# Attention scores of an encoder trunk: three products of 96 rows, or one of 32 and two of 128

## The chip, the cores and the metric

The kernel runs on one core of one Trainium2 chip. The metric is the device time of one execution in microseconds, as a median over runs. The core has five engines that follow their own instruction streams and meet at semaphores: TensorE (PE in the profile, with its weight loads as PEld), VectorE (DVE), ScalarE (ACT), GpSimd (POOL) and SyncE (SP), which here only issues transfers. TensorE reads its operands from SBUF and writes to PSUM, of which a core has eight banks of 128 partitions by 512 float32 values.

## The reference

Two layers act on a residual stream of 512 rows and 1024 columns. Each layer normalises, projects, runs three mixers side by side (latent attention, pooling, gating), projects back, and ends with a gated feed-forward part. The change touches the attention mixer alone:

```
s = (jnp.einsum('bqhd,bkhd->bhqk', qn, k_nope)
     + jnp.einsum('bqhr,bkr->bhqk', qr, k_rope))
p = jax.nn.softmax(s.astype(jnp.float32) * scale, axis=-1).astype(v.dtype)
return jnp.einsum('bhqk,bkhd->bqhd', p, v)
```

There are 8 heads. A score is a sum over 96 terms: 64 of a part without position (`nope`, its own key for each head) and 32 of a rotated part (`rope`, one key that all heads share). Queries go in four blocks of 128, keys are 512.

## The kernel before, in words

**Two parts for each number.** Operands of TensorE are split into a high part (rounded to the type `float32r`) and a low part (the rest). A product of two split operands takes three passes: high by high, high by low, low by high (`mm3`, line 538). A tile that holds both parts is a "unit" of 128 partitions, two slots and 512 columns, named `u` in the profile.

**Attention before the change.** `pair(pr)` makes the keys and queries of two heads: 15 products of 128 rows, then for each head ScalarE writes the high part and VectorE the low part into partitions 0 to 63 of the head's units `kh` and `qh`, slot 0 and slot 1, and two transfers by SyncE put both parts of the rotated key and query into partitions 64 to 95. `score(i)` then handles tile `i`, that is head `i // 4` and query block `i % 4`: three passes of 96 rows into one PSUM bank, then the softmax (VectorE's maximum, ScalarE's exponential with its sum, VectorE's reciprocal, and the scaling on VectorE or GpSimd). `turn(i)` transposes the probabilities on TensorE and splits them, and `weigh(n)` multiplies two turned tiles with the values. There are 32 tiles in a layer. `AHEAD = 4`, `WLAG = 2` and `PAIR = 4` say by how many tiles these steps are written apart; other work (`BESIDE`: gating, pooling, and `out_early`, the first half of the output projection) is written between them.

**What sets the order.** Nothing is issued as it is written. A recording layer (`Program`) takes every operation down, and `order` (line 330) places them: engine by engine it takes the operation that can start earliest by its own table of costs (`_cost`, line 233) and lags, and among those the one whose successors are due first. PSUM has three pools, "s" with three banks (scores), "p" with three (turned probabilities and weighted values) and "b" with two. Operations written with `either` go to VectorE, or to GpSimd where the planner sees them end early enough there. All instructions are issued from one line (493), so the profile tells them apart by their tiles: `ps` is a PSUM bank, `t` a tile of 512 columns, `s` the softmax's small numbers, `wu` split weights, `raw` weights as loaded.

**Queues.** SyncE's transfers stand in one queue, in the planner's order: a transfer that waits for its source holds back those behind it, weight loads too.

Of the kernel before, what the change touches and what calls it, by code (L numbers as in the profile page):

```python
# [16 lines left out]
ALU = mybir.AluOpType  # L17
AX = mybir.AxisListType

P = 128  # L20
D = 1024
T = 512
NT = T // P
# [3 lines left out]
NOPE = 64  # L27
ROPE = 32
# [188 lines left out]
class Op:  # L217
# [15 lines left out]
    def _cost(self, engine):  # L233

        n = self.out.free() if isinstance(self.out, View) else 0
        if self.method == "tensor_reduce":
            n = max(x.free() for x in self.reads)
        if self.method == "dma_start":
            return 1.0 if engine == "gpsimd" else 0.06
        if engine == "tensor":  # L240
            return {1: 0.213, P: 0.109}.get(n, n / 2400 + 0.0135)
        vectors = sum(isinstance(self.kw.get(k), View) for k in ("bias", "scale", "scalar", "scalar1", "accum_out"))
        from_psum = any(x.buf.pool.psum for x in self.reads)
        if engine == "scalar":
            return (0.05 if from_psum else 0.09) + n / 1200 + 0.093 * vectors
        if engine == "gpsimd":
            if self.kw.get("op") == ALU.pow:
                return 0.3 + n * 0.165
            return 0.15 + n * 0.0021 if self.method == "tensor_tensor" else 0.05 + n * 0.0013
        if self.method == "reciprocal":  # L250
            return 0.08 + n * 0.008
        fast = self.method in ("tensor_copy", "tensor_scalar") and not from_psum
        return 0.07 + n / (1920 if fast else 960) + 0.06 * vectors
# [245 lines left out]
def encoder(ctx: ExitStack, tc: tile.TileContext, wts, xT, pos, cols, sgn, fin, cst, rc, out):  # L499
    nc = Program(tc)  # L500
# [34 lines left out]
    def f32(ap):  # L535
        return ap.bitcast(F32)
# [167 lines left out]
    for l in range(DEPTH):  # L704
# [213 lines left out]
        def k_rotary():  # L918
            wr = unit()[:, 0].rearrange("p (k c) -> p k c", c=2 * ROPE)
            raw = load(l, 8)  # L920
            rraw = raw[:, : KD * ROPE].rearrange("p (k c) -> p k c", c=ROPE)
            nc.scalar.activation(wr[:, :, :ROPE], rraw, AF.Copy)
            nc.vector.tensor_tensor(out=wr[:, :, ROPE:], in0=rraw, in1=f32(wr[:, :, :ROPE]), op=ALU.subtract)
            rot_parts["w"] = split(raw, 768, None, 256)
            ps = bank("b")
            for k in range(KD):
                nc.tensor.matmul(ps[: 2 * ROPE], wr[:, k], xg[k][:, 0], start=(k == 0), stop=False)
                nc.tensor.matmul(ps[: 2 * ROPE], wr[:, k], xg[k][:, 1], start=False, stop=(k == KD - 1))
            kr = tmp()
            nc.scalar.copy(out=kr[:ROPE], in_=ps[ROPE : 2 * ROPE])  # L930
            nc.vector.tensor_tensor(out=kr[:ROPE], in0=kr[:ROPE], in1=ps[:ROPE], op=ALU.add)
            nc.vector.tensor_tensor(out=kr[:ROPE], in0=kr[:ROPE], in1=rs["bc"][:ROPE], op=ALU.mult)
            rot_parts["k"] = rotate(kr, ROPE)

        def rotate(src, n):

# [93 lines left out]
        def pair(pr):  # L1030
            w = weights(l, 14 + pr, nc.either)
            pk = bank("b")
            for k in range(KKV):
                s = slice(k * P, (k + 1) * P)
                mm3(pk[:], w[:, 0, s], w[:, 1, s], ckv[k][:, 0], ckv[k][:, 1], k == 0, k == KKV - 1)
            pq = bank("b")
            for k in range(KQ):
                s = slice((KKV + k) * P, (KKV + k + 1) * P)
                mm3(pq[:], w[:, 0, s], w[:, 1, s], cq[k][:, 0], cq[k][:, 1], k == 0, k == KQ - 1)
            for j in range(2):  # L1040
                h = 2 * pr + j
                kh, qh = unit(), unit()
                rows = slice(j * NOPE, (j + 1) * NOPE)
                for dst, src in ((kh, pk), (qh, pq)):
                    nc.scalar.activation(dst[:NOPE, 0], src[rows], AF.Copy)
                    nc.vector.tensor_tensor(
                        out=dst[:NOPE, 1], in0=src[rows], in1=f32(dst[:NOPE, 0]), op=ALU.subtract
                    )
                nc.sync.dma_start(f32(kh[NOPE:E]), f32(rot_parts["k"][:ROPE]))
                qrow = slice((h % 4) * ROPE, (h % 4 + 1) * ROPE)  # L1050
                nc.sync.dma_start(f32(qh[NOPE:E]), f32(qrot[h // 4][qrow]))
                heads[h] = (kh, qh)

        probs, pts = {}, {}

        def score(i):
            h, t = divmod(i, NT)
            kh, qh = heads[h]
            ts_ = slice(t * P, (t + 1) * P)
            ps = bank("s")  # L1060
            mm3(ps[:], qh[:E, 0, ts_], qh[:E, 1, ts_], kh[:E, 0], kh[:E, 1], True, True)
            st = small("att")
            nc.vector.tensor_reduce(out=st[:, 0:1], in_=ps[:], axis=AX.X, op=ALU.max, negate=True)
            pe = tmp()
            nc.scalar.activation(pe[:], ps[:], AF.Exp, bias=st[:, 0:1], accum_out=st[:, 2:3])
            nc.vector.reciprocal(out=st[:, 3:4], in_=st[:, 2:3])
            nc.either.tensor_scalar(
                out=pe[:], in0=pe[:], scalar1=st[:, 3:4], scalar2=1.0, op0=ALU.mult, op1=ALU.mult
            )
            probs[i] = pe  # L1070

        def turn(i):
            pe = probs.pop(i)
            if i % 2 == 0:
                pth, ptl = unit(), unit()
                pts[i // 2] = [x[:].rearrange("p a (k q) -> p (a k) q", q=256) for x in (pth, ptl)]
            pth3, ptl3 = pts[i // 2]
            pt = bank("p")
            for kt in range(NT):
                nc.tensor.transpose(pt[:, kt * P : (kt + 1) * P], pe[:, kt * P : (kt + 1) * P], ident[:])  # L1080
            pt3 = pt[:].rearrange("p (k q) -> p k q", q=P)
            qs = slice((i % 2) * P, (i % 2 + 1) * P)
            nc.scalar.activation(pth3[:, :, qs], pt3, AF.Copy)
            nc.vector.tensor_tensor(out=ptl3[:, :, qs], in0=pt3, in1=f32(pth3[:, :, qs]), op=ALU.subtract)

        fulls = {}

        def weigh(n):
            h, qp = divmod(n, 2)
            pth3, ptl3 = pts.pop(n)  # L1090
            po = bank("p")
            for kt in range(NT):
                nc.tensor.matmul(po[:, :256], vt[kt][:, h], pth3[:, kt], start=(kt == 0), stop=False)
# [40 lines left out]
        for i in range(max(n_tiles + AHEAD + WLAG, max(BESIDE) + 1)):  # L1134
            if i < n_tiles:
                if i % 8 == PAIR and i // 8 + 1 < HEADS // 2:
                    pair(i // 8 + 1)
                score(i)
            j = i - AHEAD
            if 0 <= j < n_tiles:  # L1140
                turn(j)
            for name in BESIDE.get(i, ()):
                jobs[name]()
            j = i - AHEAD - WLAG
            if j >= 0 and j % 2 == 1:
                weigh(j // 2)


        acc = tpool.tile([P, T], F32, tag="acc", name=nm("acc"), bufs=2)
# [555 lines left out]
```

## Time and profile before

| | us |
|---|---|
| median of 3 runs | 1097.53 (1097.27 to 1097.63) |
| the profiled execution's own time | 1096.46 |
| its span, first to last instruction | 1094.7 |
| attention of the first layer, first to last score | 92.7 to 167.1 |
| attention of the second layer | 635.4 to 709.8 |

The profile is one execution. Its page gives each engine's busy time; matmuls are pipelined and their ends are modelled, so a busy TensorE is not one at its peak, and the pace of products is read from the starts of groups in the timeline. A row of a groups view has the line, engine, operation and tiles, count, busy time, mean of one, and what the engine waited for ahead of it. A row of the windows view has the stretch, then for each engine its busy time and instructions.

### The profile page before, as it was taken

How to read it: one execution, taken by the hardware profiler on the slowest of the kernel's cores; microseconds unless marked ns; L12 is line 12 of the kernel's file. 1: busy time of each engine (PE TensorE's matmuls, PEld its weight loads, DVE VectorE, ACT ScalarE, POOL GpSimd, SP SyncE). 2: the span in 40 equal slices, each digit the busy share in tenths (PEclk: the TensorE clock that was granted, in tenths of full speed). 3: DMA queues.
4: the chain of work that ended last, by engine and by line, in shares of the span. 5: the costliest groups of instructions: out<-in, count | busy, mean ns of one | idle time of the engine just before them, and what ended most of it. 6: DMA issues, size and time to landing. Idle time of an engine off the chain costs nothing.

```text
span 1094.7 us, 14521 instructions
## 1 busy us (share of the span) xinstructions
PE 1070.3 (98%) x5324; PEld 900.6 (82%) x5324; DVE 864.6 (79%) x1196; ACT 648.8 (59%) x995; POOL 170.5 (16%) x198
## 2 busy tenths in 40 slices
PE   9999899999999999999999998999999999999997
PEld 7787688888888999887887877888888889998885
DVE  7679996898876778994556899969977866799963
ACT  6357784775565555662353677847755655666642
POOL 0217320101001100020001273201001001100201
PEclk9999999999999999999999999999999999999999
DMA  6333214656546547385132422155567356563922
GB/s 214 101 100 94 69 44 152 190 148 141 140 131 134 118 133 227 101 221 130 58 116 75 129 66 63 59 203 144 157 151 172 97 126 144 137 209 102 259 64 97
DMA packets 44392, 142.71 MB, mean 130 GB/s; under 512 B 5744, under 2 KB 6000, under 8 KB 44320
## 3 DMA queue, kind: packets, MB, share of 16 engines
q1 hardware_dynamic: 33936, 108.05, 29.7%
q0 software_dynamic: 9808, 32.67, 16.9%
q10 hardware_dynamic: 576, 1.05, 0.3%
q8 instruction: 42, 0.69, 0.2%
q14 instruction: 30, 0.25, 0.1%
HBM read 135.33 MB, written 2.23 MB: 126 GB/s over the span
## 4 chain that ended last, share of the span: by engine, by line
PE 84%; DVE 8%; issue 4%; ACT 3%; DMA 1%; POOL 1%; POOLq 0%; DVEq 0%; ACTq 0%
PE ps L493 84%; DVE u L493 4%; DVE t L493 2%; DVE s L493 1%; ACT u L493 1%; ACT t L493 1%; DVE wu L493 1%; ACT wu L493 1%; DMA wr<-in_wts 0%; DVE vz L493 0%; DMA u<-u 0%; ACT vm L493 0%; DVE z L493 0%; POOL u L493 0%; POOL r L493 0%
## 5 line engine op out<-in xcount | busy, mean ns | idle before, releaser
L493 PE MATMUL ps<-wu,xp 128*128 128x512 f32 (+1 forms) x2976 | 658.7, 380 | 2.4 <-ACT wu L493 2.0
L493 PEld LDWEIGHTS ps<-wu,xp 128*128 128x128 f32 x2976 | 547.0, 188 | 93.0 <-ACT wu L493 2.3
L493 ACT ACTIVATE wu<-wr 128x1024 fp32r<-128x1024 f32 (+1 forms) x224 | 225.3, 1008 | 200.1 <-PE ps L493 162.6
L493 DVE TENSOR_TENSOR wu<-wr,wu 128x1024 fp32r<-128x1024 f32 (+1 forms) x224 | 258.3, 1156 | 92.2 <-ACT wu L493 91.4
L493 PE MATMUL ps<-u,wu 128*128 128x512 f32 x972 | 236.6, 395 | 2.5 <-DVE wu L493 1.7
L493 PEld LDWEIGHTS ps<-u,wu 128*128 128x128 f32 x972 | 178.6, 188 | 42.3 <-DVE wu L493 3.2
L493 POOL DMA_DIRECT2D wr<-in_wts x64 | 55.9, 983 | 561.5 <-DVE wr L493 201.3
L493 PE MATMUL ps<-u,u 128*128 128x256 f32 (+3 forms) x516 | 107.0, 344 | 4.2 <-ACT t L493 2.6
L493 ACT ACTIVATE wu<-raw 128x1024 fp32r<-128x1024 f32 (+3 forms) x66 | 63.1, 959 | 65.1 <-PE ps L493 40.0
L493 ACT COPY t<-ps 128x512 f32<-128x512 f32 (+3 forms) x124 | 62.2, 503 | 47.5 <-PE ps L493 43.9
L493 PEld LDWEIGHTS ps<-u,u 128*128 128x128 f32 (+2 forms) x516 | 74.6, 186 | 18.3 <-ACT t L493 4.3
L493 DVE TENSOR_TENSOR wu<-raw,wu 128x1024 fp32r<-128x1024 f32 (+3 forms) x60 | 67.6, 1130 | 27.1 <-ACT wu L493 26.6
L493 DVE TENSOR_TENSOR wr<-wr,wr 128x1024 f32<-128x1024 f32 (+1 forms) x64 | 73.7, 1154 | 4.8 <-DMA wr<-in_wts 4.4
L493 DVE TENSOR_TENSOR u<-ps,u 128x512 fp32r<-128x512 f32 (+1 forms) x104 | 70.0, 683 | 6.1 <-ACT u L493 5.1
L493 ACT ACTIVATE u<-ps 128x512 fp32r<-128x512 f32 (+1 forms) x104 | 61.2, 596 | 15.6 <-PE ps L493 14.3
L493 DVE TENSOR_TENSOR t<-ps,t 128x512 f32<-128x512 f32 (+2 forms) x92 | 50.4, 567 | 20.7 <-PE ps L493 16.2
L493 ACT ACTIVATE t<-ps,s 128x512 f32<-128x512 f32 x64 | 43.8, 688 | 9.4 <-DVE s L493 7.8
L493 POOL TENSOR_SCALAR t<-t,s 128x512 f32<-128x512 f32 x54 | 37.8, 705 | 66.1 <-DVE s L493 49.6
L493 PE MATMUL ps<-ident,t 128*128 128x128 f32 x288 | 43.7, 274 | 4.0 <-DVE t L493 2.1
L493 PEld LDWEIGHTS ps<-ident,t 128*128 128x128 f32 x288 | 34.0, 140 | 15.1 <-issue 5.0
L493 DVE TENSOR_TENSOR res<-ps,res 128x512 f32<-128x512 f32 x40 | 27.6, 689 | 21.6 <-PE ps L493 21.3
L493 DVE TENSOR_REDUCE s<-ps 128x1 f32<-128x512 f32 x64 | 42.4, 679 | 0.8 <-PE ps L493 0.6
(129 smaller groups left out, 804.5 us busy)
## 6 DMA issues: line engine op xcount, KB each, us to landing
wr<-in_wts SPq DMA_DIRECT2D x104, 512.0 KB, 4.5
raw<-in_wts SPq DMA_DIRECT2D x50, 512.0 KB, 3.5
wr<-in_wts POOLq DMA_DIRECT2D x48, 512.0 KB, 5.5
wr<-in_wts SPq DMA_DIRECT2D x32, 384.0 KB, 3.2
wr<-in_wts POOLq DMA_DIRECT2D x16, 384.0 KB, 4.8
u<-u SPq DMA_DIRECT2D x32, 128.0 KB, 2.3
raw<-in_wts SPq DMA_DIRECT2D x8, 320.0 KB, 3.1
res<-in_xT SPq DMA_DIRECT2D x8, 256.0 KB, 5.2
```

What stands on the lines that cost most here:

```text
L493: getattr(getattr(nc, op.engine), op.method)(*[real(x) for x in op.args], **{k: real(x) for k, x in op.kw.items()})
```

## The change

The three passes of 96 rows become two of 128 and one of 32. Slot 0 of a head's units now holds: the high `nope` part (64 rows), the rotated key's high part twice (32 and 32), and against it the rotated query's high and low part. Slot 1 holds the key's low and high `nope` part, and against it the query's high and low part in the opposite order. So the first pass of 128 rows gives high by high of `nope` and both products with the rotated key's high part, the second gives the two mixed products of `nope`. What is left, the rotated query's high part by the rotated key's low part, is a product of 32 rows that reads the rotated tiles where they lie: partitions 32 times (head modulo 4), for which the rotated key's low part is copied to all four groups of 32 partitions.

Tiles go in another order: the two heads of a pair take turns (`tile_of`), and `scores` writes both 32-row products, of two heads and so in two row groups, ahead of the four passes. Both heads of a pair are therefore wanted at its first two tiles. Each head now has six transfers (two copies of a high part of 64 rows, four of 32 rows) where it had two; with three for the key's low part there are 51 in a layer where there were 16. The planner's cost of a 32-row product is set to n / 4800 + 0.0135, some half of that of another.

```
+            if self.reads and self.args and self.args[1].shape[0] == ROPE:
+                return n / 4800 + 0.0135
...
-            rot_parts["k"] = rotate(kr, ROPE)
+            rot_parts["k"] = u = rotate(kr, ROPE)
+            for x in range(1, 4):
+                nc.sync.dma_start(f32(u[x * ROPE : (x + 1) * ROPE, 1]), f32(u[:ROPE, 1]))
...
-                for dst, src in ((kh, pk), (qh, pq)):
+                low, high = slice(0, NOPE), slice(NOPE, P)
+                for dst, src, rest, again in ((kh, pk, low, high), (qh, pq, high, low)):
                     nc.scalar.activation(dst[:NOPE, 0], src[rows], AF.Copy)
+                    nc.sync.dma_start(f32(dst[again, 1]), f32(dst[:NOPE, 0]))
                     nc.vector.tensor_tensor(
-                        out=dst[:NOPE, 1], in0=src[rows], in1=f32(dst[:NOPE, 0]), op=ALU.subtract
+                        out=dst[rest, 1], in0=src[rows], in1=f32(dst[:NOPE, 0]), op=ALU.subtract
                     )
-                nc.sync.dma_start(f32(kh[NOPE:E]), f32(rot_parts["k"][:ROPE]))
                 qrow = slice((h % 4) * ROPE, (h % 4 + 1) * ROPE)
-                nc.sync.dma_start(f32(qh[NOPE:E]), f32(qrot[h // 4][qrow]))
+                for x in range(2):
+                    at = slice(NOPE + x * ROPE, NOPE + (x + 1) * ROPE)
+                    nc.sync.dma_start(f32(kh[at, 0]), f32(rot_parts["k"][:ROPE, 0]))
+                    nc.sync.dma_start(f32(qh[at, 0]), f32(qrot[h // 4][qrow, x]))
...
-            mm3(ps[:], qh[:E, 0, ts_], qh[:E, 1, ts_], kh[:E, 0], kh[:E, 1], True, True)
...
+        def tile_of(i):
+
+            return i // 8 * 2 + i % 2, i % 8 // 2
+
+        def scores(i):
+
+            pss = [bank("s"), bank("s")]
+            for x in range(2):
+                h, t = tile_of(i + x)
+                row = slice((h % 4) * ROPE, (h % 4 + 1) * ROPE)
+                ts_ = slice(t * P, (t + 1) * P)
+                nc.tensor.matmul(pss[x][:], qrot[h // 4][row, 0, ts_], rot_parts["k"][row, 1], start=True, stop=False)
+            for x in range(2):
+                h, t = tile_of(i + x)
+                kh, qh = heads[h]
+                ts_ = slice(t * P, (t + 1) * P)
+                for y in range(2):
+                    nc.tensor.matmul(pss[x][:], qh[:, y, ts_], kh[:, y], start=False, stop=(y == 1))
+                soften(i + x, pss[x])
```

`turn` and `weigh` follow the new order of tiles; their work is the same. The counts of TensorE, ScalarE and VectorE-or-GpSimd operations are the same.

**TensorE, in the first layer's third pair.** Before, a tile is one group of three passes (here with its head's units `u_986` and `u_1307`):

```order
L493 MATMUL ps_1493<-ident,t_1334 128x128 x4
L493 MATMUL ps_1499<-u_986,u_1307 128x512 x3
L493 MATMUL ps_1507<-ident,t_1353 128x128 x4
L493 MATMUL ps_1518<-u_555,wu_1294 128x512 x2
L493 MATMUL ps_1523<-u_1471,u_903 128x256
```

Now the two 32-row products (with the rotated key `u_473` and query `u_1290`) stand ahead of the passes of two heads:

```order
L495 MATMUL ps_1491<-ident,t_1379 128x128 x4
L495 MATMUL ps_1500<-u_473,u_1290 128x512
L495 MATMUL ps_1502<-u_473,u_1290 128x512
L495 MATMUL ps_1500<-u_1133,u_1302 128x512 x2
L495 MATMUL ps_1509<-u_1370,u_915 128x256
```

They are neighbours here. In the second pair (rotated query `u_901`), tile by tile, they are not:

```order
L495 MATMUL ps_1175<-u_473,u_901 128x512
L495 MATMUL ps_1175<-u_854,u_911 128x512 x2
L495 MATMUL ps_1190<-u_473,u_901 128x512
L495 MATMUL ps_1190<-u_866,u_913 128x512 x2
L495 MATMUL ps_1198<-u_473,u_901 128x512
L495 MATMUL ps_1198<-u_854,u_911 128x512
```

Of the 64 products of 32 rows in the program, 26 stand as 13 such neighbours (8 in the first layer, 5 in the second) and 38 stand alone, with a pass or a transpose on either side.

**SyncE, at the first layer's first and second pair.** Before, four transfers (rotated query `u_882` to the units of four heads) and one of the key for the next pair:

```order
L493 DMA raw_893<-in_wts 128x640
L493 DMA u_866<-u_882 32x1024
L493 DMA u_876<-u_882 32x1024
L493 DMA u_938<-u_882 32x1024
L493 DMA u_940<-u_882 32x1024
L493 DMA u_986<-u_473 32x1024
```

Now, for the same heads (`u_881`, `u_885`, `u_911`, `u_913`), the copies of the high parts and the rotated parts, with a weight load between them:

```order
L495 DMA u_881<-u_881 64x512
L495 DMA u_885<-u_885 64x512
L495 DMA u_881<-u_901 32x512
L495 DMA u_885<-u_901 32x512
L495 DMA u_911<-u_901 32x512
L495 DMA u_913<-u_901 32x512
L495 DMA raw_924<-in_wts 128x640
L495 DMA u_881<-u_901 32x512
L495 DMA u_885<-u_901 32x512
```

The rotated parts now need two transfers a head, and the copies that wait for ScalarE stand in the same queue.

**GpSimd, late in the first layer's attention.** Before, it scales probabilities (`t` by `s`):

```order
L493 TENSOR_SCALAR t_1515<-t_1515,s_1504 128x512
L493 TENSOR_SCALAR t_1533<-t_1533,s_1521 128x512
L493 TENSOR_SCALAR t_1590<-t_1590,s_1580 128x512
L493 TENSOR_SCALAR t_1609<-t_1609,s_1597 128x512
L493 TENSOR_SCALAR t_1638<-t_1638,s_1627 128x512
```

Now it also takes low parts of weights of `out_early`, 1024 columns each:

```order
L495 TENSOR_SCALAR t_1527<-t_1527,s_1514 128x512
L495 TENSOR_TENSOR wu_1583<-raw_1547,wu_1583 128x1024
L495 TENSOR_SCALAR t_1608<-t_1608,s_1593 128x512
L495 TENSOR_SCALAR t_1628<-t_1628,s_1614 128x512
L495 TENSOR_SCALAR t_1658<-t_1658,s_1646 128x512
L495 TENSOR_SCALAR t_1681<-t_1681,s_1667 128x512
L495 TENSOR_TENSOR wu_1722<-raw_1664,wu_1722 128x1024
```

Over the program, seven such subtractions of 1024 columns move from VectorE to GpSimd, three of them in each layer's attention.

More of the change, by code (lines that the diff above doesn't have):

```diff
@@ L1043, in pair, with soften @@
                 rows = slice(j * NOPE, (j + 1) * NOPE)
-                for dst, src in ((kh, pk), (qh, pq)):
+                low, high = slice(0, NOPE), slice(NOPE, P)
+                for dst, src, rest, again in ((kh, pk, low, high), (qh, pq, high, low)):
                     nc.scalar.activation(dst[:NOPE, 0], src[rows], AF.Copy)
+                    nc.sync.dma_start(f32(dst[again, 1]), f32(dst[:NOPE, 0]))
                     nc.vector.tensor_tensor(
-                        out=dst[:NOPE, 1], in0=src[rows], in1=f32(dst[:NOPE, 0]), op=ALU.subtract
+                        out=dst[rest, 1], in0=src[rows], in1=f32(dst[:NOPE, 0]), op=ALU.subtract
                     )
-                nc.sync.dma_start(f32(kh[NOPE:E]), f32(rot_parts["k"][:ROPE]))
                 qrow = slice((h % 4) * ROPE, (h % 4 + 1) * ROPE)
-                nc.sync.dma_start(f32(qh[NOPE:E]), f32(qrot[h // 4][qrow]))
+                for x in range(2):
+                    at = slice(NOPE + x * ROPE, NOPE + (x + 1) * ROPE)
+                    nc.sync.dma_start(f32(kh[at, 0]), f32(rot_parts["k"][:ROPE, 0]))
+                    nc.sync.dma_start(f32(qh[at, 0]), f32(qrot[h // 4][qrow, x]))
                 heads[h] = (kh, qh)
         probs, pts = {}, {}
[L1056 to L1060, printed above, removed]
-            mm3(ps[:], qh[:E, 0, ts_], qh[:E, 1, ts_], kh[:E, 0], kh[:E, 1], True, True)
+        def tile_of(i):
[14 more added lines that the diff above has]
+                soften(i + x, pss[x])
+        def soften(i, ps):
             st = small("att")
@@ L1073, in turn @@
             pe = probs.pop(i)
-            if i % 2 == 0:
+            h, t = tile_of(i)
+            if t % 2 == 0:
                 pth, ptl = unit(), unit()
-                pts[i // 2] = [x[:].rearrange("p a (k q) -> p (a k) q", q=256) for x in (pth, ptl)]
-            pth3, ptl3 = pts[i // 2]
+                pts[h, t // 2] = [x[:].rearrange("p a (k q) -> p (a k) q", q=256) for x in (pth, ptl)]
+            pth3, ptl3 = pts[h, t // 2]
             pt = bank("p")
@@ L1081, in turn @@
             pt3 = pt[:].rearrange("p (k q) -> p k q", q=P)
-            qs = slice((i % 2) * P, (i % 2 + 1) * P)
+            qs = slice((t % 2) * P, (t % 2 + 1) * P)
             nc.scalar.activation(pth3[:, :, qs], pt3, AF.Copy)
@@ L1086, in encoder, with weigh @@
         fulls = {}
-        def weigh(n):
-            h, qp = divmod(n, 2)
-            pth3, ptl3 = pts.pop(n)
+        def weigh(h, qp):
+            n = h // 2 * 4 + qp * 2 + h % 2
+            pth3, ptl3 = pts.pop((h, qp))
             po = bank("p")
@@ L1137, in encoder @@
                     pair(i // 8 + 1)
-                score(i)
+                if i % 2 == 0:
+                    scores(i)
             j = i - AHEAD
@@ L1144, in encoder @@
             j = i - AHEAD - WLAG
-            if j >= 0 and j % 2 == 1:
-                weigh(j // 2)
+            if j >= 0 and j % 4 >= 2:
+                h, t = tile_of(j)
+                weigh(h, t // 2)
         acc = tpool.tile([P, T], F32, tag="acc", name=nm("acc"), bufs=2)
```

## The prediction

> **What bounds the kernel now.** I read the busy times first, then the windows view to cut the span into stages, then the chain of waits within the attention of the first layer. Two stages hold the changed products; the rest of the span issues the same work as before.
>
> ```profile
> span 1094.7 us, 14521 instructions
> PE 1070.3 (98%) x5324; PEld 900.6 (82%) x5324; DVE 864.6 (79%) x1196; ACT 648.8 (59%) x995; POOL 170.5 (16%) x198
> ```
>
> ```profile
> 92.70:167.10 74.40, 70.42 (x401) 57.11 (x402) 68.97 (x137) 58.86 (x130) 34.67 (x38) 1.00 0.23 66
> 635.40:709.80 74.40, 69.86 (x401) 57.00 (x402) 69.35 (x137) 58.08 (x129) 33.69 (x37) 1.00 0.22 65
> ```
>
> The columns are the stretch and its length, then busy time and instructions of TensorE, its weight loads, VectorE, ScalarE and GpSimd, then the granted clock, the share of the DMA engines and GB/s. Over the program TensorE is the bound (98%). In attention it is not alone: of 74.4 us it is busy 70.4 and VectorE 69.0. Finer stretches of the first layer's attention show that the two take turns:
>
> ```profile
> 92.70:102.70 10.00, 10.00 (x49) 8.07 (x50) 9.56 (x20) 8.04 (x19) 9.66 (x9) 1.00 0.34 94
> 102.70:112.70 10.00, 9.22 (x55) 7.12 (x54) 9.91 (x20) 8.13 (x18) 5.56 (x7) 1.00 0.22 59
> 112.70:122.70 10.00, 8.62 (x47) 6.65 (x45) 9.42 (x20) 8.95 (x20) 2.78 (x3) 1.00 0.03 7
> 122.70:132.70 10.00, 8.54 (x53) 6.75 (x51) 9.77 (x21) 7.77 (x18) 5.25 (x7) 1.00 0.58 168
> 132.70:142.70 10.00, 9.90 (x62) 8.42 (x61) 7.38 (x15) 6.97 (x15) 3.70 (x5) 1.00 0.01 2
> 142.70:152.70 10.00, 9.75 (x60) 7.67 (x59) 9.85 (x20) 8.08 (x19) 2.78 (x4) 1.00 0.17 52
> 152.70:167.10 14.40, 14.40 (x87) 12.43 (x86) 13.08 (x27) 10.92 (x25) 4.93 (x6) 1.00 0.24 75
> ```
>
> From 102.7 to 132.7 TensorE has holes (9.22, 8.62, 8.54 of 10) and VectorE almost none. The chain that ended last says the same: the first row below is its share by line from 102.7 to 132.7, the second from 152.7 to 167.1.
>
> ```profile
> by line: DVE u L493 24.8%; ACT u L493 16.1%; DVE s L493 16.0%; ACT t L493 9.1%; issue 8.2%; PE ps L493 7.5%; DVE t L493 5.9%; ACT wu L493 5.3%; POOL u L493 4.3%; ACT vm L493 2.4%; DVE vz L493 1.2%; ACTq L493 0.2%
> by line: PE ps L493 101.8%
> ```
>
> So 30 of the 74 us belong to VectorE and ScalarE (TensorE 7.5% of the chain), and time that TensorE saves there is worth nothing. About 44 us (92.7 to 102.7 and 132.7 to 167.1) are TensorE's, the stretch from 142.7 shared with VectorE. The second layer has the same sums, and I take it to be alike.
>
> **The change: the products.** A layer has 32 tiles of three 96-row passes. The next rows are timeline rows: start, length, tiles, count.
>
> ```profile
> 85.73 5.60 PE L493 MATMUL ps<-wu,u 128*128 128x512 f32 x24
> 91.17 1.29 PE L493 MATMUL ps<-u,wu 128*128 128x512 f32 x5
> 97.90 0.86 PE L493 MATMUL ps<-u,u 96*128 96x512 f32 x3
> 98.60 0.60 PE L493 MATMUL ps<-ident,t 128*128 128x128 f32 x4
> ```
>
> From group start to group start, 24 passes of 128 rows take 91.17 - 85.73 = 5.44 us, 0.227 each; three of 96 rows take 98.60 - 97.90 = 0.70, 0.233 each. So a pass costs by its columns and not by its rows, and three instructions for three save nothing alone, save for the 0.006 us: 192 times that is 1.2 us at most, and as I trust a third digit little and 40% of it lies in VectorE's stretches, I take 0.4.
>
> The gain must come from two 32-row products that run side by side. In the planned order only 13 of the 32 possible couples are neighbours; 38 products stand alone and then cost a whole 0.227, as the pass before them did. For a couple, no row of before shows two products in one time, so the price is bounded. Without overlap it saves 0. For the best case I look for the closest start behind another:
>
> ```profile
> 161.38 0.60 PE L493 MATMUL ps<-ident,t 128*128 128x128 f32 x4
> 161.74 2.98 PE L493 MATMUL ps<-u,wu 128*128 128x512 f32 x12
> 171.47 1.04 PE L493 MATMUL ps<-ident,t 128*128 128x128 f32 x8
> 172.26 3.02 PE L493 MATMUL ps<-u,wu 128*128 128x512 f32 x12
> ```
>
> Eight transposes and the start behind them take 0.79 us, four take 0.36. The four more are 0.108 each, and the start behind the last comes 0.36 - 3 x 0.108, some 0.03 later. A second product 0.03 behind the first saves 0.20. But the 0.108 is itself a price: a transpose has 128 columns of weights and 128 to stream where a pass streams 512 in 0.227, so its pace should be that of the weight load, and a second product that waits for one starts 0.108 behind and saves 0.119. I take 0.119, since each of the two brings its own weights, the same 128 columns, and weight loads come one after another. [...]
>
> Of the 13 couples, three in the first layer and two or so in the second fall where VectorE is as busy as TensorE (the stretch from 142.7); I count these half and so take ten: 10 x 0.119 = **1.2 us saved** (0 to 2.6 for 13 at 0.20).
>
> **VectorE.** Each head still has one subtraction for the low part of key and query, of the same size. But the planner moves other work: three weight subtractions of 1024 columns in each layer's attention from VectorE to GpSimd.
>
> ```profile
> L493 DVE TENSOR_TENSOR wu<-raw,wu 128x1024 fp32r<-128x1024 f32 x4 | 4.9, 1219 | 0.2 <-ACT wu L493 0.2
> L493 POOL TENSOR_TENSOR wu<-raw,wu 128x640 fp32r<-128x640 f32 x2 | 3.1, 1567 | 5.9 <-ACT wu L493 5.9
> 143.52 1.21 DVE L493 TENSOR_TENSOR wu<-raw,wu 128x1024 fp32r<-128x1024 f32 x1
> 155.61 1.23 DVE L493 TENSOR_TENSOR wu<-raw,wu 128x1024 fp32r<-128x1024 f32 x1 [0.17 <-ACT wu L493]
> 161.35 1.22 DVE L493 TENSOR_TENSOR wu<-raw,wu 128x1024 fp32r<-128x1024 f32 x1
> ```
>
> On VectorE one is 1.22 us. GpSimd takes 1.57 for 640 columns, some 2.5 for 1024, on an engine that is busy 4.93 of 14.4 us there. Of the three, those at 155.61 and 161.35 lie where TensorE is full, and save nothing; the one at 143.52 lies where VectorE is busy 9.85 of 10. Bounds for both layers: 0 to 2.4 us; I take **0.8 saved**, since TensorE has 9.75 of the same 10.
>
> **The transfers and the second head.** These speak against the change.
>
> ```profile
> L493 SPq DMA_DIRECT2D u<-u x9: 507/528/577, 92.2 to 124.3; - x9
> u<-u SPq DMA_DIRECT2D x32, 128.0 KB, 2.3
> 92.68 1.16 PE L493 MATMUL ps<-u,u 96*128 96x512 f32 x4 [0.21 <-DMA u<-u]
> ```
>
> SyncE needs 0.528 us to issue one and it lands 2.3 us after its issue. A pair has 12 instead of 4, so the last is issued 8 x 0.528 = 4.2 us later; bytes are no matter at a DMA share of 0.23. A high part for the second pass is now copied (0.5 + 2.3 us) after ScalarE has written it, where the low part came from VectorE directly. And the second head is wanted four tiles, 4 x 74.4 / 32 = 9.3 us, earlier. Behind a TensorE pass that waits for its copy stand, in program order, the transposes of other tiles and a product of `out_early`; behind those VectorE's next splits. What hides it: `pair` is written four tiles ahead, and between the last product of the pair and the first pass that needs it the new order puts transposes, weighings and `out_early` products. Bounds: 0, or one whole copy (2.8 us) at each of the six changes of pair, 16.8 us. At the first scores of a layer the transfers already end last before (0.21 us at 92.68), so it is not free: I take **0.7 lost**.
>
> Sum: 0.4 + 1.2 + 0.8 - 0.7 = 1.7 us less. Against the profiled execution's 1096.46 (span 1094.7 and 1.8 around it) that is 1094.8. The median of the runs is 1.07 above that execution, so for the median I forecast 1097.53 - 1.7 = **1095.8**, own range 1093.8 to 1097.2.
>
> **The rivals.**
>
> *More than that.* Couples start 0.03 apart (2.6 us), and the lighter VectorE counts whole (2.4) with 0.4 for the pace: 5 us, **1092.5**. For it: from 142.7 both engines are full and both get less. Against: 38 products alone.
>
> *It does not do what it says.* The second of a couple needs its own bank, one of three, and waits for ScalarE's exponential to free it; then the couple is neighbours in the order but not in time. Saved is the pace alone, and the transfers take that back: **1097.5**. For it: the planner itself kept 38 of 64 apart.
>
> *Slower, at the change of pair.* One mechanism: the copy for the second pass lands after TensorE has run out of other work. Its place is the first tiles of the second, third and fourth pair. It decides once the cover is shorter than 0.5 + 2.3 us and the transfers queued ahead. At a whole copy for the last pair of both layers, where TensorE is the bound (5.6 us), and 0.3 at the four others, it is 6.8 lost for the 0.7 above: **1102**. For it: 70 more issues of 0.528. Against: DMA share 0.03 and 0.01 in two stretches.
>
> *A price for changing the shape.* If TensorE must run empty whenever the row count changes, entering and leaving each of the 51 groups (13 couples, 38 alone) costs a product's length less its pace.
>
> ```profile
> L493 PE MATMUL ps<-u,u 96*128 96x512 f32 x95 | 28.9, 413 | 1.9 <-ACT t L493 1.0 <-ACT u L493 0.7 <-DMA u<-u 0.2
> 36.90 3.84 PE L493 MATMUL ps<-u,u 128*64 128x512 f32 x16
> 40.57 1.75 PE L493 MATMUL ps<-u,wu 128*128 128x512 f32 x7
> ```
>
> That is 0.413 - 0.233 = 0.18, and 102 x 0.18 = 18 us; 60% of it counts: +11, less the gains, **1107**. The 64-column products are the nearest row against it: 16 of them, entered from and left to full ones, take 40.57 - 36.90 = 3.67 us, 0.229 each, so that entering and leaving cost 16 x 0.002, some 0.04. [...]
>
> **How the numbers follow.** A measurement of this kernel can tell 0.2%, 2.2 us, from no change, so faster means under 1095.3. Chances: the forecast 0.50, of which 0.22 fall under 1095.3 and 0.28 within; more gain 0.18; not what it says 0.13, of which 0.03 above 1099.7; the change of pair 0.14; the price for shape 0.05. That makes faster 0.40, same 0.38, slower 0.22. The range reaches from 1091.5, one below the rival with more gain, to 1101.5, which leaves out the shape price and half of the slower rival.
>
> **What would show it.** Couples: timeline rows of 32-row products in twos, the next group 0.33 us behind the first for a start 0.108 apart, 0.26 for 0.03, 0.45 for none. Lone ones: 0.227 to the next pass; more means a price for shape. Attention by windows: each layer's 74.4 us should be 73 to 74; TensorE's waits for `u<-u` should stay under 1 us in all. Wrong would be: a wait for a transfer of over 1 us at a change of pair, or a stage outside attention that moves by over 1 us.

## The result, and the profile after

| | before | after |
|---|---|---|
| median of 6 runs each, same chip | 1097.82 us (1097.27 to 1098.78) | 1114.07 us (1110.08 to 1116.69) |
| profiled execution | 1096.46 us | 1113.62 us |
| its span | 1094.7 us | 1111.8 us |

The change made the kernel slower: the ratio of the times is 1.0143, with a 95% interval of 1.0118 to 1.0167. That is 16.3 us more, where 1.7 less were forecast, and outside the range.

Where it went, by stretches of the span: up to the last score of the first layer 174.2 us instead of 167.1 (+7.1), from there to the last score of the second layer 550.7 instead of 542.7 (+8.0), and the rest 386.9 instead of 384.9 (+2.0). The windows view of after, each layer's attention from first to last score, and then ten microseconds of the first (columns as in the prediction's rows):

```profile
88.20:174.20 86.00, 81.65 (x416) 61.00 (x416) 72.72 (x143) 62.18 (x136) 42.40 (x40) 0.96 0.29 82
641.30:724.90 83.60, 81.11 (x416) 59.34 (x416) 74.85 (x148) 62.05 (x136) 39.43 (x36) 1.00 0.33 89
...
112.70:122.70 10.00, 9.62 (x32) 6.55 (x32) 7.71 (x17) 5.96 (x16) 3.54 (x5) 0.66 0.11 34
```

The stretches took 86.0 and 83.6 us instead of 74.4. TensorE is busy over 81 us in both, instead of 70, with almost the same number of products (416 instead of 401, since scores begin somewhat earlier). The last row shows something that the attention of before does not have: a mean granted clock of 0.66.

VectorE and ScalarE have nearly the same work as before, and VectorE holds up less of the span: in the chain of waits that ended last, by engine, first of before and then of after, its share falls from 8% to 5%, and TensorE's rises from 84% to 87%.

```profile
PE 84%; DVE 8%; issue 4%; ACT 3%; DMA 1%; POOL 1%; POOLq 0%; DVEq 0%; ACTq 0%
```

```profile
PE 87%; DVE 5%; issue 4%; ACT 2%; DMA 1%; POOL 0%; SPq 0%; POOLq 0%; ACTq 0%; DVEq 0%
```

How a 32-row product goes is best seen in the timeline around one couple of the first layer, of TensorE's products and then of its weight loads (start, length, what; in brackets the idle time ahead and what ended it):

```profile
148.92 0.39 PE L495 MATMUL ps<-u,wu 128*128 128x512 f32 x1
149.24 0.50 PE L495 MATMUL ps<-u,u 32*128 32x512 f32 x2
```

```profile
149.24 0.18 PEld L495 LDWEIGHTS ps<-u,u 32*128 32x128 f32 x2 [0.35 <-issue]
149.67 0.77 PEld L495 LDWEIGHTS ps<-u,u 128*128 128x128 f32 x4 [0.25 <-issue]
```

The two 32-row products share one row of 0.50 us: the trace has their starts 0.003 to 0.004 us apart, and so it is in 12 of the 13 couples. By the starts the overlap is complete. But the couple begins 0.32 us behind the pass ahead of it, not 0.227, and the next pass can begin only at 149.67, 0.43 later. In both places the weight load stands idle first (0.35 and 0.25) and then starts together with its product. Among equal passes of before, weight loads run beside the product ahead: of three passes that start from 97.90 on, two load their weights from 97.91 on.

```profile
97.91 0.42 PEld L493 LDWEIGHTS ps<-u,u 96*128 96x128 f32 x2
```

"issue" says that it waited for nothing that the profile shows. The starts in the trace give the same for nearly all of the 51 groups: some 0.09 us more on the way in, 0.20 on the way out, and 0.11 more for the pass after that, whose weight load starts 0.11 us behind the pass ahead of it (149.77 and 149.67), where that of equal passes starts with it (97.91 and 97.90). Together that is **0.405 us for a product that stands alone**, and 0.405 - 0.223 = 0.18 for a couple, which has one product's length less. The sum, 38 x 0.405 + 13 x 0.18, is 17.7 us of TensorE's time.

The page's group of weight loads of before and of after carries the same sign, 39.8 us idle instead of 18.3:

```profile
L493 PEld LDWEIGHTS ps<-u,u 128*128 128x128 f32 (+2 forms) x516 | 74.6, 186 | 18.3 <-ACT t L493 4.3
```

```profile
L495 PEld LDWEIGHTS ps<-u,u 128*128 128x128 f32 (+2 forms) x516 | 75.2, 190 | 39.8 <-issue 17.5
```

### The profile page after: what moved, and what is told of

Same layout as the page of the kernel before. It is cut to its first block, busy times and chain, and to the rows that moved or that the text cites. A ratio compares the mean times of both kernels' runs of the same rounds, so it can differ in the third digit from the quotient of the medians.

```text
span 1111.8 us, 14684 instructions
## 1 busy us (share of the span) xinstructions
PE 1088.3 (98%) x5324; PEld 902.7 (81%) x5324; DVE 865.6 (78%) x1192; ACT 649.8 (58%) x995; POOL 191.1 (17%) x202
## 4 chain that ended last, share of the span: by engine, by line
PE 87%; DVE 5%; issue 4%; ACT 2%; DMA 1%; POOL 0%; SPq 0%; POOLq 0%; ACTq 0%; DVEq 0%
PE ps L495 87%; DVE u L495 1%; DVE wu L495 1%; ACT u L495 1%; ACT wu L495 1%; DVE t L495 1%; DMA raw<-in_wts 1%; DMA wr<-in_wts 0%; ACT t L495 0%; DMA u<-u 0%; DVE xp L495 0%; DVE s L495 0%; DVE xs L495 0%; DVE vz L495 0%; DVE wr L495 0%
## 5 line engine op out<-in xcount | busy, mean ns | idle before, releaser
L495 PE MATMUL ps<-u,u 128*128 128x256 f32 (+3 forms) x516 | 118.0, 367 | 5.9 <-DVE u L495 1.6
L495 PEld LDWEIGHTS ps<-u,u 128*128 128x128 f32 (+2 forms) x516 | 75.2, 190 | 39.8 <-issue 17.5
L495 DVE TENSOR_TENSOR wu<-raw,wu 128x1024 fp32r<-128x1024 f32 (+3 forms) x53 | 59.9, 1134 | 23.3 <-ACT wu L495 22.8
L495 ACT ACTIVATE u<-ps 128x512 fp32r<-128x512 f32 (+1 forms) x104 | 60.8, 595 | 19.0 <-PE ps L495 17.7
```

What stands on the lines that cost most here:

```text
L495: getattr(getattr(nc, op.engine), op.method)(*[real(x) for x in op.args], **{k: real(x) for k, x in op.kw.items()})
```

## The experiments

My theory was now "shape": a change of row count costs TensorE 0.405 us for each group of 32-row products, whatever runs side by side. The rivals were the transfers and the second head's lateness, the new order of tiles, and the half clock. Times below are medians against the kernel before on the same chip.

**Two kernels without 32 rows, two with other groupings.** In `one_size` the third product has 128 rows:

```
-nc.tensor.matmul(pss[x][:], qrot[h // 4][row, 0, ts_], rot_parts["k"][row, 1], start=True, stop=False)
+nc.tensor.matmul(pss[x][:], qrot[h // 4][:, 0, ts_], rot_parts["low"][h % 4], start=True, stop=False)
```

> The changed kernel, but its third product has 128 rows as well: the rotated key's low part lies in one of four row groups of a tile that is zero elsewhere, and is multiplied with all 128 rows of the rotated query. No product of 32 rows is left; order of tiles, transfers and second head stay as changed. Theory 'shape' (a group of 32-row products costs 0.405 us when one product stands alone and 0.18 when two do, for TensorE is empty while the row count changes): the loss is gone, 1096 to 1100. Theory 'transfers' (the second head or its copies come late): the loss stays, 1110 or more, with TensorE waiting for copies. Theory 'order' (heads that take turns upset the planned order): the loss stays, 1108 or more. Theory 'clock' (more rows at work lower the granted clock): all passes now have 128 rows, so half-speed stretches stay or grow, 3.4 us each, 1101 or more.

Measured 1109.78 us against 1099.39, ratio 1.0097 (1.0082 to 1.0112). `couples` makes the planner place the two 32-row products of `scores` next to each other:

```
+first, second = nc.ops[-2:]
+first.glued, second.follows = second, True
```

> The changed kernel with the planner told to place the two 32-row products of a pair of tiles as neighbours always: 32 couples, none alone, instead of 13 and 38. Theory 'shape': the groups cost 32 x 0.18 = 5.8 us instead of 38 x 0.405 + 13 x 0.18 = 17.7; of that some 70% reaches the end, as in the changed kernel, so 1101 to 1105; the gain is less if the second PSUM bank comes late. Theories 'transfers' and 'order': nothing of either is changed, 1110 to 1116. Within a couple the second product starts 0.003 to 0.004 us behind the first.

Measured 1114.38, ratio 1.0131 (1.0115 to 1.0148). `alone` writes each 32-row product with its own tile:

```
-            for x in range(2):
-                h, t = tile_of(i + x)
-                ts_ = slice(t * P, (t + 1) * P)
```

> The changed kernel with each 32-row product written with its own tile: 60 stand alone and 2 couples are left, so 62 groups for 51. Theory 'shape': 60 x 0.405 + 2 x 0.18 = 24.7 us instead of 17.7, 70% of it at the end: 1115 to 1121. Theories 'transfers' and 'order': as the changed kernel, 1110 to 1116.

Measured 1127.29, ratio 1.0253 (1.0238 to 1.0268). `turns` is the kernel before in the new order of tiles:

```
-    h, t = divmod(i, NT)
+    return i // 8 * 2 + i % 2, i % 8 // 2
```

> The kernel before (three passes of 96 rows, its transfers) with the changed order of tiles alone: the heads of a pair take turns, so that both are wanted at its first two tiles. Theory 'shape': no change, 1096 to 1100. Theory 'order': most of the loss, 1106 or more. Theory 'transfers': a part of the loss, since the second head is wanted early but has its 4 transfers instead of 12 for a pair: 1100 to 1106, with TensorE waiting for copies at a change of pair.

Measured 1111.15, ratio 1.0109 (1.0094 to 1.0124). The four are ordered as "shape" says: 60 lone groups and 2 couples take 17.5 us more than the same kernel in one size, 32 couples 4.6 more. But all four lie 6 to 11 us above the ranges that "shape" had given them, and `one_size` and `turns` lie where "order" had them. Both kernels without a change of row count stayed 10.4 and 11.8 us above before, so "shape" was not all. Nor does a couple in the order stay one in time: in `couples` 27 of the 32 second products start 0.003 to 0.004 us behind the first, and five start 0.4 to 2.1 us behind it. In the first layer of `turns` the timeline shows where TensorE stands still, and the windows view what follows:

```profile
97.41 0.93 PE L493 MATMUL ps<-u,u 128*128 128x512 f32 x3 [1.95 <-DVE u L493]
102.60 5.29 PE L493 MATMUL ps<-u,u 96*128 96x512 f32 x12 [4.25 <-DMA u<-u]
```

```profile
100.60:107.50 6.90, 4.90 (x12) 3.81 (x12) 6.29 (x12) 3.00 (x5) 0.00 (x0) 0.51 0.84 210
```

TensorE waits 4.25 us for a copy at the first scores, and from 100.6 to 107.5 the granted clock is 0.51: the twelve products from 102.60 take 5.29 us, where 12 x 0.233 are 2.8. So the slow products behind the stall take some 2.5 us more. The second layer of `turns` has a standstill too, 6.4 us long (in the waits view below: us in total, times, longest), and from within it on the trace has half the clock for 13.65 us.

```profile
PE ps L493 <- issue: 6.4, 1, 6.4
```

**The new transfers, in the old order of tiles.** `heads` is `one_size` with the tiles head after head; `alone_heads` is the changed kernel's products in that order.

```
-def scores(i):
-    pss = [bank("s"), bank("s")]
+def score(i):
+    h, t = divmod(i, NT)
```

> The kernel of the run one_size (third product with 128 rows, all transfers of the change), but with the tiles in the order of before: head after head, one tile at a time. Theory 'order' (heads that take turns bunch VectorE's work at the start of attention, so TensorE waits and its clock is halved for a few microseconds): the loss of one_size is gone, within 2 us of before. Theory 'transfers' (the copies themselves come late): the loss stays, 8 us or more over before.

> The changed kernel's products, 64 of them with 32 rows, but with the tiles in the order of before, so that each stands alone. Theory 'shape': 64 x 0.405 = 25.9 us of TensorE's time, of which VectorE's stretches hide 30 to 40%: 15 to 19 us over before, with little loss by waits and clock. If only the order mattered: within 2 us of before.

Measured: `heads` 1108.95 against 1099.33, ratio 1.0094 (1.0079 to 1.0109); `alone_heads` 1122.30, ratio 1.0214 (1.0197 to 1.0231). The 64 products of 32 rows cost 13.4 us over `heads`, and `alone_heads` is 23.0 us above before, where 15 to 19 were expected. The heads' taking turns is not the cause of the other 10, since `heads` has them too; "transfers" seemed right. On the chain of waits of `heads` in the second layer there was in fact a weight load (`raw`) that SyncE had issued behind eight copies and the load of a table:

```profile
635.28 4.70 DMA raw<-in_wts
```

**Which part of the transfers?** Three edits of `heads`, in this order: the copies issued by ScalarE (`heads_queue`), the copies replaced by a second write of ScalarE (`heads_write`), and the third product repeating the first, without the zero tiles (`again`).

```
-nc.sync.dma_start(f32(dst[again, 1]), f32(dst[:NOPE, 0]))
+nc.scalar.dma_start(f32(dst[again, 1]), f32(dst[:NOPE, 0]))
...
-nc.sync.dma_start(f32(dst[again, 1]), f32(dst[:NOPE, 0]))
+nc.scalar.activation(dst[again, 1], src[rows], AF.Copy)
...
-nc.tensor.matmul(ps[:], qrot[h // 4][:, 0, ts_], rot_parts["low"][h % 4], start=True, stop=False)
+nc.tensor.matmul(ps[:], qh[:, 0, ts_], kh[:, 0], start=True, stop=False)
```

> The kernel of the run heads (no 32-row products, tiles in the order of before, the transfers of the change, 9.6 us over before), with the copies of the high parts issued by ScalarE, behind its own write, and no longer by SyncE. Theory 'queue' (SyncE waits for ScalarE's write at each copy, and weight loads stand behind it): the loss falls under 4 us, and no weight load stands on the chain of waits in attention. Theory 'copies' (a copy's own 2 us behind ScalarE's write is late for the second pass): the loss stays at 8 us or more. Theory 'room' (the two zero tiles take room from others): the loss stays at 8 us or more.

> The kernel of the run heads with the second high part written by ScalarE from PSUM, 0.6 us each, instead of a copy: 16 transfers fewer in a layer, 9.6 us more on ScalarE. Theories 'queue' and 'copies': the loss of 9.6 us falls under 4. Theory 'room': it stays at 8 us or more.

> The kernel of the run heads without the zero tiles and the copies of the rotated key's low part: the third product of a tile repeats the first (128 rows), so the scores leave out the rotated key's low part and count the first products twice. Theories 'queue' and 'copies': the loss stays at 8 us or more. Theory 'room': within 3 us of before.

Measured against 1097.90: `heads_queue` 1110.07, ratio 1.0105 (1.0085 to 1.0124); `heads_write` 1103.92, 1.0051 (1.0036 to 1.0066); `again` 1103.17, 1.0052 (1.0036 to 1.0069). "Queue" fell. The other two lie between the bounds of every theory, 6.0 and 5.3 us above before where `heads` had 9.6: each edit seemed to take away 4 us or so, by two unlike means. That spoke for two costs, or for something that every edit shares: the planner makes a new order for the whole program after each.

**Is it the order itself?** `again_write` has both edits. `replan_a` and `replan_b`, in this order below, are the kernel before with a number of the planner changed, and no operation (the planner moves four operations from GpSimd to VectorE in the one, and one in the other).

```
+if self.reads and self.args and self.args[1].shape[0] == 96:
+    return n / 2400 + 0.05
...
-LEAD = 140
+LEAD = 144
```

> The kernel of the run again (third product repeats the first, no zero tiles; the scores leave out the rotated key's low part), and the second high part written by ScalarE instead of a copy, as in heads_write. Each of the two edits took 4 to 5 us off the loss of heads. Theory 'two costs' (copies and room cost separately): within 2 us of before. Theory 'other order' (the planner's order of before fits the chip better than any that it makes after an edit, whichever): 3 us or more over before.

> The kernel before, and only the planner's table says 0.0365 us more for a 96-row product, so that it orders the same instructions a little differently (about 5% of TensorE's rows move). Theory 'other order': 3 us or more over before, with waits for VectorE and ScalarE in attention and stretches at half clock. Theory 'two costs': within 2 us of before.

> The kernel before, and only the planner's rule on how many products ahead a tile may be claimed is 144 instead of 140: the same instructions, about 8% of TensorE's rows moved. Theory 'other order': 3 us or more over before. Theory 'two costs': within 2 us of before.

Measured against 1099.38: `again_write` 1113.16, ratio 1.0133 (1.0118 to 1.0148); `replan_a` 1099.61, 1.0008 (0.9996 to 1.0021); `replan_b` 1108.50, 1.0094 (1.0074 to 1.0113). "Two costs" fell outright: both edits together lose more than either. And a new order alone costs 0.2 us in one case and 9.1 in the other, with the same operations and the same transfers. So "other order", which had said 3 us or more for both, missed `replan_a` and had `replan_b` right: some new orders cost as much, and not every one. The timeline of `replan_b` at the first scores of both layers, and its windows view around the first of these, show where the 9.1 us lie:

```profile
98.32 0.94 PE L493 MATMUL ps<-u,u 128*128 128x512 f32 x3 [1.94 <-DVE u L493]
103.41 6.74 PE L493 MATMUL ps<-u,u 96*128 96x512 f32 x15 [4.16 <-DMA u<-u]
...
652.38 4.07 PE L493 MATMUL ps<-u,u 96*128 96x512 f32 x9 [6.44 <-issue]
```

```profile
89.70:99.70 10.00, 7.61 (x33) 5.68 (x31) 9.06 (x16) 5.58 (x10) 9.01 (x5) 1.00 0.00 0
99.70:109.90 10.20, 6.49 (x15) 4.99 (x16) 9.65 (x16) 5.15 (x11) 1.24 (x3) 0.51 0.55 150
109.90:119.90 10.00, 10.00 (x68) 8.97 (x67) 9.06 (x22) 9.78 (x26) 7.00 (x7) 0.99 0.17 46
```

It is the stall of `turns`, at the same place and almost of the same lengths, and from 99.7 on 10.2 us have half the clock. Ahead of the last products the half-clock stretches in the traces of `replan_b` and of `turns` add up to 23.9 us each, where before has 3.4, which can be up to 10 us of time (an estimate, half of the difference). So the loss of `turns` says nothing certain on heads that take turns, and that of `heads` nothing certain on transfers: each of these kernels has an order of its own, and orders differ by as much. The 17.5, 4.6 and 13.4 us above are differences across two orders as well.

**The change of row count, free of a new order.** `cut` and `cut_half` keep the order of before row by row on every engine. Only the third product of each tile, or of each second tile, reads fewer rows:

```
-mm3(ps[:], qh[:E, 0, ts_], qh[:E, 1, ts_], kh[:E, 0], kh[:E, 1], True, True)
+nc.tensor.matmul(ps[:], qh[:E, 0, ts_], kh[:E, 0], start=True, stop=False)
+nc.tensor.matmul(ps[:], qh[:E, 0, ts_], kh[:E, 1], start=False, stop=False)
+nc.tensor.matmul(ps[:], qh[:ROPE, 1, ts_], kh[:ROPE, 0], start=False, stop=True)
```

> The kernel before, in its own order, row by row on every engine; only the third product of each tile reads the first 32 of its 96 rows (64 rows of each score's third product are left out). So 64 products of 32 rows stand alone, and nothing else moves. Theory 'shape': 64 x 0.405 = 25.9 us of TensorE's time; VectorE's stretches (40% of attention) hide their part, so 14 to 19 us over before, and the weight load of the product behind starts 0.4 us behind the 32-row product. Theory 'other order' alone (all of the loss comes from the new order): within 2 us of before.

> As cut, but only every second tile has its third product cut to 32 rows: 32 groups instead of 64. Theory 'shape': 32 x 0.405 = 13 us of TensorE's time, and about half of what cut loses, 6 to 10 us. Theory 'other order' alone: within 2 us of before.

Measured against 1098.06: `cut` 1116.83, ratio 1.0173 (1.0158 to 1.0188), `cut_half` 1105.39, ratio 1.0070 (1.0053 to 1.0087). A third of the scores' products have fewer rows to multiply, and the kernel is 18.8 us slower; with half as many such products, 7.3. That is 0.29 and 0.23 us for each of 64 and 32 groups, out of 0.405. I take the rest to lie beside waits for VectorE that were there anyway; that was not measured by itself. The clock is a small part of it: ahead of the last products before has half the clock for 3.4 us, `cut` for 10.2 and `cut_half` for 6.8; half of what is added, 3.4 and 1.7 us, is an estimate of what it can have cost. The groups view of `cut`, weight loads of 32 rows (the last figures are their idle time in all, and what ended it):

```profile
L493 PEld LDWEIGHTS ps<-u,u 32*128 32x128 f32 x64 | 11.6, 181 | 22.5 <-issue 22.0 <-DVE u L493 0.2
```

Each stands idle for 22.5 / 64 = 0.35 us, as the couple's in the changed kernel, and nothing visible holds it.

**The price by itself.** `probe` is the kernel before with 328 products behind its last one, which the 1181.73 us of its one execution include:

```
+for pattern in (lone, couple, four, same, half, halves, most, narrow, only):
+    for _ in range(12):
+        full()
+    for _ in range(8):
+        pattern()
```

> The kernel before, with short patterns of products on TensorE added at its end, whose results nobody reads; each pattern eight times, with twelve whole products (128 rows, 512 columns) between patterns. In microseconds from one pattern's start to the next. Theory 'shape' (the count of rows must change): one whole product and one of 32 rows 0.75 (0.32 in, 0.43 out); with two of 32 rows in two row groups 0.75, with four in four 0.76; with two in the same row group 0.98; with one or two of 64 rows 0.75; a whole one and one of 96 rows 0.454; a whole one and one of 64 columns 0.454; four of 32 rows with no whole one between, 0.23 for the four. Theory 'weights' (what costs is that weights for other rows are not loaded ahead, at each product that is not whole): the 96-row pattern costs 0.75 too, and the four alone cost more than 0.23. Theory 'chance' (the intervals in the changed kernel come from waits for operands): 0.454 for every pair and 0.23 less for the ones side by side.

The timeline of `probe`, some rows of each pattern in this order: one product of 32 rows between whole ones; two in two row groups; four in four; two in the same group; one of 64 rows; two of 64 rows in two row groups; whole ones and 96 rows by turns; whole ones and 64 columns by turns; four of 32 rows with no whole one between.

```profile
1093.00 0.50 PE L516 MATMUL probe_s<-xp,xp 128*128 128x512 f32 x1
1093.43 0.49 PE L519 MATMUL probe_s<-xp,xp 32*128 32x512 f32 x1
1093.85 0.49 PE L516 MATMUL probe_s<-xp,xp 128*128 128x512 f32 x1
...
1109.08 0.50 PE L516 MATMUL probe_s<-xp,xp 128*128 128x512 f32 x1
1109.51 0.50 PE L519 MATMUL probe_s<-xp,xp 32*128 32x512 f32 x1
1109.52 0.49 PE L519 MATMUL probe_p<-xp,xp 32*128 32x512 f32 x1
1109.94 0.50 PE L516 MATMUL probe_s<-xp,xp 128*128 128x512 f32 x1
...
1115.28 0.50 PE L516 MATMUL probe_s<-xp,xp 128*128 128x512 f32 x1
1115.71 0.49 PE L519 MATMUL probe_s<-xp,xp 32*128 32x512 f32 x1
1115.71 0.50 PE L519 MATMUL probe_p<-xp,xp 32*128 32x512 f32 x3
1116.14 0.50 PE L516 MATMUL probe_s<-xp,xp 128*128 128x512 f32 x1
...
1125.21 0.50 PE L516 MATMUL probe_s<-xp,xp 128*128 128x512 f32 x1
1125.64 0.73 PE L519 MATMUL probe_s<-xp,xp 32*128 32x512 f32 x2
1126.30 0.50 PE L516 MATMUL probe_s<-xp,xp 128*128 128x512 f32 x1
...
1140.89 0.50 PE L516 MATMUL probe_s<-xp,xp 128*128 128x512 f32 x1
1141.33 0.50 PE L519 MATMUL probe_b<-xp,xp 64*128 64x512 f32 x1
1141.76 0.50 PE L516 MATMUL probe_s<-xp,xp 128*128 128x512 f32 x1
...
1152.00 0.51 PE L516 MATMUL probe_s<-xp,xp 128*128 128x512 f32 x1
1152.44 0.50 PE L519 MATMUL probe_b<-xp,xp 64*128 64x512 f32 x2
1152.87 0.49 PE L516 MATMUL probe_s<-xp,xp 128*128 128x512 f32 x1
...
1161.18 3.90 PE L516 MATMUL probe_s<-xp,xp 96*128 96x512 f32 x16
...
1167.65 3.87 PE L516 MATMUL probe_s<-xp,xp 128*64 128x512 f32 x16
...
1174.51 0.39 PE L519 MATMUL probe_s<-xp,xp 32*128 32x512 f32 x1
1174.52 0.39 PE L519 MATMUL probe_p<-xp,xp 32*128 32x512 f32 x2
1174.75 0.39 PE L519 MATMUL probe_s<-xp,xp 32*128 32x512 f32 x1
```

A whole product and one of 32 rows take 1093.85 - 1093.00 = 0.85 us instead of 0.454, and the same with two or four side by side (0.86 and 0.86) or with one or two of 64 rows (0.87 both). I had expected 0.75: here every whole product stands right behind a change and right ahead of the next, and starts 0.42 to 0.43 us behind the one ahead, as does the next behind it. The changed kernel has this at 96.73 too: products of 32 rows start 0.43 us ahead of a whole one and 0.43 behind it, and its weight load starts together with it. With 96 rows by turns sixteen products go through at 3.90 / 16, under 0.25 (the 3.90 hold the whole length of the last one; from start to start the trace has 0.234), with 64 columns at the same pace, and four of 32 rows follow four of 32 rows 0.24 behind (1174.75 - 1174.51). So in these runs the price is for the change to 32 or 64 rows and back; 96 rows count as a whole product, and 64 columns beside 128 cost nothing. "Weights" fell with the 96 rows, "chance" with all of it. Two products in the same row group are 1.09 a pattern: the second costs 0.23 more.

## Why the prediction was wrong, point by point

**The step that failed: "38 products stand alone and then cost a whole 0.227".** They cost 0.227 and 0.405. The rival "a price for changing the shape" was right on where the price falls and nearly on its size: 0.18 for a switch, 0.36 for a group, against 0.405 measured; it gave 1107, and I gave it 0.05. That TensorE runs empty, as it says, the runs can't show, since the ends of products are modelled; they show weight loads that stand idle and start with their own product. I put the rival aside for the 64-column products, entered and left for 0.04 us. That row was read rightly, and `probe` repeats it, but it changes columns, while the change alters rows. The row that I had for rows, 96 beside 128, was no change of shape either, as the same run shows. No row of before bore on 32 rows, and a cost that no row bounds should have kept the chance of its rival, and an end of the range.

What `probe` shows is a price of some 0.4 us for a group, for 32 and for 64 rows beside 128 (0.85 and 0.87 us with the whole one, against 0.454). A change of columns (16 products in 3.87 us), or from 96 to 128 rows (16 in 3.90), showed none.

**Couples.** In 12 of the 13 the starts are 0.003 to 0.004 us apart, and in the one shown above the weight loads too (149.236 and 149.239). The 0.108 that I took for a second weight load was too pessimistic: that weight loads come one after another was my own estimate, from transposes. The closer start was of no use by itself: a couple saves 0.223 and its group costs 0.405.

**What reached the end.** The rival counted 60% of the price. By `cut` it is 18.8 / 25.9, some 73%. At that share the changed kernel's 17.7 us give 12.9 of the 16.3 measured. This is worked out across two orders, and not measured in one.

**The rest, some 3 us, and the term that was missing.** The sum took for granted that whatever the edit did not touch would stay in place. The planner made a new order, and a new order alone cost 0.2 us in one run and 9.1 in another. None of the new orders tried was faster than that of before. I can't say how the 3 us divide between order, transfers and clock: the kernels that were to tell it had orders of their own, and the two edits that each lowered the loss of `heads` raised it to 13.8 when put together. The 2.0 us of the last stage, which the prediction had named as a sign of being wrong, go with 8 more products in it (1834 instead of 1826 in the windows view).

**Transfers (0.7 lost).** Not settled, for that reason. A late weight load is now on the chain of waits of after, where before had none:

```profile
90.16 3.22 DMA raw<-in_wts
```

I had counted copies that land late for TensorE, and not the weight loads queued behind them, though SyncE has one queue. What this load cost is small as far as it can be seen: TensorE waited 0.7 us for it (the last figure of the groups row below), and `cut`, with the transfers of before, has a weight load on its chain too. The rival at the change of pair did not come: all waits of TensorE's score passes for copies are 1.0 us in the program, as the groups view of after has it (last figures):

```profile
L495 PE MATMUL ps<-u,u 128*128 128x512 f32 x140 | 49.5, 442 | 1.8 <-DMA u<-u 1.0 <-DMA raw<-in_wts 0.7
```

**VectorE (0.8) and the pace (0.4).** Neither can be seen. The moves to GpSimd happened, and TensorE is busy 11 us longer in each layer's attention, so that VectorE sets less of its length. It still sets some: in this row of after VectorE is busy 9.91 of 10 us and TensorE 7.50.

```profile
102.70:112.70 10.00, 7.50 (x41) 5.00 (x40) 9.91 (x16) 6.89 (x15) 4.49 (x6) 1.00 0.32 90
```

In `probe` whole products and ones of 96 rows by turns start 0.234 us apart, 0.007 more than the 0.227 of whole ones in before: about what I had read, and too little to matter.

**The clock.** I had left it out, as the rows of attention before show 1.00. In after the stretch from 112.7 has 0.66, that is 6.8 us at half speed and at most 3.4 us lost. Another such 6.8 us begin at 418.7, where before has 3.4 us at 410.7, so that some 5 of the 16.3 us can be the clock's (an estimate, half of the difference); how far it makes up the rest above is open. The times go with it: the six executions of after reach from 1110.08 us with a mean granted clock of 0.999 to 1116.69 with 0.990. The first, a single one, has hardly any half clock and is still 12.3 us above the median of before, near the 12.9 worked out for the products.

## What to carry to other kernels

In these runs rows left free in TensorE were not free to use: a 32- or 64-row product between whole ones cost 0.4 us on top of its own time (0.85 to 0.87 against 0.454 in `probe`), so such products have to stand in long runs (four behind four take 0.24), or at least four in four row groups together (0.86 us with the whole one, against 5 x 0.227), or be filled up to whole ones. Where a planner orders the work, compare an edit with a kernel whose order is the same (`cut`), and measure first what a new order alone costs (`replan_b`); otherwise differences of 1% are explained by whatever was edited. And when a row is used to rule a rival out, ask whether it varies the same thing.

Whether groups of four would beat the kernel before was not tried: by the figures above they save at most 16 x 0.28 = 4.5 us (an estimate), and a new order may cost more.

## What I had not expected of the hardware

TensorE's clock halved behind a few microseconds in which it was mostly idle: in `replan_b`, with waits of 1.94 and 4.16 us, 10.2 us have 0.51 from within the second wait on; in `turns`, with 1.95 and 4.25, it is 6.9 us. But it also halved without such waits. In after the half clock begins at 115.0, and in the 6.8 us ahead the longest wait is 1.6 us; in `probe` TensorE is busy without a hole by the profile, with whole products and ones of 32 rows by turns, and has half the clock all the same (by windows, from 1091.7 to 1098.5 it is busy 6.80 of 6.80 us at a clock of 1.00, and from 1098.5 to 1105.3 again 6.80, at 0.50; in the timeline the product of 32 rows that starts at 1098.55 takes 0.79 us, and those ahead of it 0.49 or 0.50). The rows of `probe` shown further above all lie outside such stretches. Ahead of the program's last products, the half-clock stretches last 3.41 us in before, 6.83 twice in after, 10.2 in `replan_b`'s first layer and 13.65 in the second of `turns`, all whole multiples of 3.41. What sets them off, these runs do not show.

And side by side means different row groups: in `probe` two 32-row products in the same group took 1.09 us with the whole one, 0.23 more than two in two groups (0.86), and four in four groups start within 0.01 us of each other.
